# A buffer of its own for the experts' weighted rows, and the gate's Silu and product scheduled with priority

## The chip, the cores and the metric

The kernel runs on one core of a Trainium2 chip. The metric is the device time of one execution in microseconds (us), as the median of several runs. One execution was also profiled; all rows below come from that one.

## The reference, cut to what matters

The layer is a mixer (attention and a chunked recurrence) followed by an expert-choice mixture of experts. Only the experts matter here:

```python
# one of 16 experts e; each takes its own 128 tokens (the context's share included)
xe   = h2[idx[e]]                       # gather 128 rows of 1024
hid  = silu(xe @ w_gate[e]) * (xe @ w_up[e])     # 1024 x 1024 each
y    = (hid @ w_down[e]) * gate[e] * g2          # 1024 x 1024
acc.at[idx[e]].add(y)                   # scatter-add into the residual stream
```

All of it is float32. TensorE multiplies in a reduced form, so the kernel splits each operand into a high and a low part and forms three products (high by high, high by low, low by high).

## The kernel before, in words

The stage of the experts runs from about 1090 to 1680 us of the span. For each expert e, `up(e)` brings in four pairs of 1 MB pieces of `w_gate` and `w_up`, and `down(e-1)` four pieces of `w_down`: 12 loads of 1 MB per expert, all on SyncE's queue (L1469), each into a slot `raw` of a ring of 16 (RING 9, MORE 6 and one of the router's). Each piece holds two 128x1024 slices. For each slice ScalarE copies the high part `whi` (L1475) and VectorE subtracts to get the low part `wlo` (L1476), so that an expert needs 24 of each. The five `whi` and five `wlo` buffers (WHI, WLO) are the whole distance by which these two engines can run ahead of TensorE.

TensorE does 144 matmuls of 128x512 columns per expert: 96 into the PSUM banks `pgu` and `pgv` (the gate's and the up product), 48 into `py` (the down product), each triple by `mm3` (L172 high by high, L173 with the low part of the rows, L174 with the low part of the weights). Beside them it transposes the gathered rows `xe` of the next expert (8 transposes L1493 into `ptm`, then `xTh` on ScalarE, L177, and `xTl` on VectorE, L178) and the hidden rows `hid` (8 more, then `hTh` and `hTl`). `ptm` has two buffers, so four transposes must be read out by VectorE before the next four but four can start.

When `pgu` is complete, ScalarE writes Silu of it into `hid` (L1520, two halves), and VectorE multiplies by `pgv` (L1521, two halves). `pgu` has one buffer: the next expert's first matmul waits for that Silu. When `py` is complete, VectorE forms the weighted rows `y` (L1540), and GpSimd scatter-adds them to DRAM (L1541). Here `y` shares its one buffer with `hid` (YT): Silu of an expert may write only when the scatter of the preceding `y` has read it, and `y` only when `hid` was transposed. GpSimd also gathers the next `xe` (L1499) and builds the `onehot` tiles for the token lists of the expert after that (L1427), which TensorE reduces in `pls` (L1430).

The order of all instructions is set by a scheduler that plays the program through ahead of time with costs of its own, and takes on each engine the next ready instruction, by priority and program order. Each engine then executes its list strictly in that order. Code under `tc.high_priority()` is taken ahead of other ready work. What can move instructions is therefore also the number of buffers, not only the priority.

Of the kernel before, what the change touches and what calls it, by code (L numbers as in the profile page):

```python
# [18 lines left out]
F32 = mybir.dt.float32  # L19
# [3 lines left out]
AF = mybir.ActivationFunctionType  # L23
ALU = mybir.AluOpType
# [4 lines left out]
P = 128  # L29
D = 1024  # L30
# [36 lines left out]
PRIO2 = 1  # L67
FPOOL = (1,)
PRIO = 1000
MORE = 6  # L70
WAIT = (16, 17, 18)
YT, RT = "hid", "xe"
WHI, WLO = 5, 5
AT = 3
QP, WP = (3,), (1, 3, 5)
XKT, WMB, LATE = (3, 4), 4, (3, 7)
# [1372 lines left out]
def _experts(K, ring, route):  # L1449
    tc, nc, a = K.tc, K.nc, K.a  # L1450
    ident = K.cst(C_IDENT)
    with tc.tile_pool(name="m", bufs=1, side="right", reuse_waits="tile") as pm, \
# [3 lines left out]
        for nm in ("hTh0", "hTl0", "hTh1", "hTl1"):  # L1456
            pm.tile([P, 4, P], F32R, name=nm)
        ring.extend((pm, MORE), (route.keep, 1))
        pm.tile([P, 2, FF], F32, name="raw", bufs=MORE)

        loads = []

        def weights(w, e, j):
            raw = ring.tile()
            loads.append(raw)
            if len(loads) in WAIT:

                nc.gpsimd.tensor_copy(raw[:, 0, 0:1], ready[0][1])
            nc.sync.dma_start(raw, w[0, e].rearrange("(k p) f -> p k f", p=P)[:, 2 * j:2 * j + 2])  # L1469
            eng = nc.gpsimd if e == 0 and (j == 0 or w is a["w_gate"] and j == 1) else nc.vector  # L1470
            his, los = [], []
            for i in range(2):
                hi = pm.tile([P, FF], F32R, name="whi", bufs=WHI)
                lo = pm.tile([P, FF], F32R, name="wlo", bufs=WLO)
                nc.scalar.activation(hi, raw[:, i], AF.Copy)  # L1475
                eng.tensor_tensor(lo, raw[:, i], hi.bitcast(F32), ALU.subtract)  # L1476
                his.append(hi)
                los.append(lo)
            return his, los
# [7 lines left out]
        def turned(src, j, nm):  # L1487

            hi, lo = (pm.tile([P, 4, P], F32R, name=f"{nm}{x}{j}") for x in "hl")
            p = ps.tile([P, 4, P], F32, name="ptm", tag="ptm", bufs=2)  # L1490
            for i in range(4):
                c = (4 * j + i) * P
                nc.tensor.transpose(p[:, i], src[:, c:c + P], ident)  # L1493
            K.split(hi, lo, p)
            return hi, lo

        def gather(e):
            xe = pm.tile([P, D], F32, name="xe")
            nc.gpsimd.indirect_dma_start(out=xe, out_offset=None, in_=K.h2_dram,  # L1499
                                         in_offset=bass.IndirectOffsetOnAxis(ap=ready[e][0][:, :1], axis=0))  # L1500
            return xe

        def up(e, xT, xe):
            pg = [ps.tile([P, FF], F32, name=nm) for nm in ("pgu", "pgv")]
            nxt = []
            for j in range(4):
                ws = [first.pop(0) if first else weights(a[w], e, j) for w in ("w_gate", "w_up")]
                for m in range(2):
                    for i in range(2):
                        k = 2 * j + i  # L1510
                        for f in range(2):
                            fs = slice(f * 512, (f + 1) * 512)
                            K.mm3(pg[m][:, fs], *(x[:, k % 4] for x in xT[k // 4]), ws[m][0][i][:, fs], ws[m][1][i][:, fs],
                                  k == 0, k == KT - 1)
                if j % 2 and xe is not None:
                    nxt.append(turned(xe, j // 2, "xT"))
            hid = pm.tile([P, FF], F32, name="hid", tag="hid" if e + 1 < NE else "xe")
            for f in range(2):
                fs = slice(f * 512, (f + 1) * 512)
                nc.scalar.activation(hid[:, fs], pg[0][:, fs], AF.Silu)  # L1520
                nc.vector.tensor_tensor(hid[:, fs], pg[1][:, fs], hid[:, fs], ALU.mult)  # L1521
            return hid, nxt

        def down(e, hT, hid=None):
# [11 lines left out]
            return py, nxt  # L1536

        def scatter(e, py):
            y = pm.tile([P, D], F32, name="y", tag=YT)
            nc.vector.scalar_tensor_tensor(y, py, ready[e][1], gt2, op0=ALU.mult, op1=ALU.mult)  # L1540
            nc.gpsimd.indirect_dma_start(out=K.acc_dram, in_=y, in_offset=None, compute_op=ALU.add,  # L1541
                                         out_offset=bass.IndirectOffsetOnAxis(ap=ready[e][0][:, :1], axis=0))

        xe = gather(0)
# [3 lines left out]
        for e in range(NE):  # L1548
            xe = gather(e + 1) if e + 1 < NE else None
            if e + 2 < NE:  # L1550
                ready.append(route.lists(e + 2, ps))
            hid, xT = up(e, xT, xe)
            if e:
                if e + 1 == NE:
                    last_hT = [turned(hid, j, "xT") for j in range(2)]
                    hid = None
                py, hT = down(e - 1, hT, hid)
                scatter(e - 1, py)
            else:
                hT = [turned(hid, j, "hT") for j in range(2)]  # L1560
# [13 lines left out]
        def norm(xs, name, pool=()):  # L1574
            ss = pm.tile([P, len(xs)], F32, name="ss" + name)
            for i, x in enumerate(xs):
                nc.scalar.activation(junk, x, AF.Square, accum_out=ss[:, i:i + 1])
            nc.vector.tensor_scalar(ss, ss, 1.0 / D, EPS, op0=ALU.mult, op1=ALU.add)
            rs = K.rsqrt(pm, ss, len(xs), tag=name)
            for i, x in enumerate(xs):  # L1580
                if i in pool:
                    nc.scalar.activation(x, x, AF.Copy, scale=rs[:, i:i + 1])
                    nc.gpsimd.tensor_tensor(x, x, g, ALU.mult)
                else:
                    nc.vector.scalar_tensor_tensor(x, x, rs[:, i:i + 1], g, op0=ALU.mult, op1=ALU.mult)
# [6 lines left out]
            for t in range(t0, t0 + n):  # L1592
                nc.sync.dma_start(out[t * P:(t + 1) * P], acc[t])
        with tc.high_priority():
            y = pm.tile([P, D], F32, name="y", tag=YT)
            nc.vector.scalar_tensor_tensor(y, py, ready[last][1], gt2, op0=ALU.mult, op1=ALU.mult)
            nc.vector.tensor_tensor(rows, rows, y, ALU.add)
            norm([rows], "r")
            nc.gpsimd.indirect_dma_start(out=out, in_=rows, in_offset=None,
                                         out_offset=bass.IndirectOffsetOnAxis(ap=ready[last][0][:, :1], axis=0))  # L1600


def body(tc, a, taps=None, stop=None):
    nc = tc.nc
    K = _K(tc, a, taps)
    with tc.tile_pool(name="const", bufs=1) as pc, tc.tile_pool(name="dram", bufs=1, space=DRAM) as dr:
# [28 lines left out]
        with contextlib.ExitStack() as banks:  # L1635
            K.gps = [banks.enter_context(tc.tile_pool(name="gps", bufs=1, space=PSUM, reuse_waits="tile"))]
            prep, left = _inproj(K, banks)
            _mix(K, prep, left)
        ring, route, keep = _outproj(K)
        _experts(K, ring, route)  # L1640
        keep.close()

# [38 lines left out]
```

## Time and profile before

| | us |
|---|---|
| median of 3 runs | 1718.07 (1716.43 to 1720.74) |
| the profiled execution | 1718.15 |
| its span | 1716.4 |
| outside the span | 1.75 |

| engine | busy us | share of the span |
|---|---|---|
| TensorE (PE) | 1528.0 | 89% |
| its weight loads (PEld) | 1298.4 | 76% |
| VectorE (DVE) | 1309.4 | 76% |
| ScalarE (ACT) | 918.6 | 54% |
| GpSimd (POOL) | 637.6 | 37% |

In the stage of the experts TensorE is busy nearly all the time and VectorE not much less; the shares of the whole span hide this, since the stages ahead have other limits. A chain of waits, read backwards from the last instruction, tells which engine sets the end: 54% of it is TensorE's. "issue" in such a chain is time in which an engine waited for nothing that the profile shows.

### The profile page before, as it was taken

What the parts mean: (1) busy time and instruction counts of PE and PEld (TensorE: products, weight loads), DVE (VectorE), ACT (ScalarE), POOL (GpSimd) and SP (SyncE); (2) the same over time, 40 slices, a digit from 0 to 9 for tenths busy, and PEclk for the clock granted to TensorE, in tenths of its full rate; (3) what the DMA queues carried; (4) which work ended last, traced back from release to release, by engine and by line L of the source; (5) the groups of instructions that cost most, each with busy time, mean ns of one, the idle gap of its engine ahead of it and who ended that gap; (6) DMA issues with size and microseconds to landing.
All of it is one profiled execution on the core that took longest, in us unless ns stands there. A gap on an engine that the chain in (4) does not pass through costs nothing.

```text
span 1716.4 us, 24735 instructions
## 1 busy us (share of the span) xinstructions
PE 1528.0 (89%) x8793; PEld 1298.4 (76%) x8793; DVE 1309.4 (76%) x2110; ACT 918.6 (54%) x1514; POOL 637.6 (37%) x555
## 2 busy tenths in 40 slices
PE   6999889899978999999898994699999999999890
PEld 2897668787867988888887784578888777777780
DVE  6656754687768877778896546789999999898884
ACT  6521125334423656556574322387777777777773
POOL 3013331322235783483710115137644335450012
PEclk9999999999988999999999997799999999999995
DMA  7477953443655043414033766799999999999915
GB/s 263 168 246 233 268 144 107 144 133 113 183 171 159 24 104 95 113 52 145 32 105 103 229 240 232 261 342 378 399 396 398 397 359 363 358 371 373 347 25 220
DMA packets 170847, 377.17 MB, mean 220 GB/s; under 512 B 32542, under 2 KB 82140, under 8 KB 169572
## 3 DMA queue, kind: packets, MB, share of 16 engines
q1 hardware_dynamic: 131874, 315.22, 50.7%
q0 software_dynamic: 11664, 43.52, 8.6%
q10 hardware_dynamic: 27186, 16.86, 3.8%
q8 instruction: 69, 1.13, 0.3%
q14 instruction: 54, 0.44, 0.1%
HBM read 315.60 MB, written 55.76 MB: 216 GB/s over the span
## 4 chain that ended last, share of the span: by engine, by line
PE 54%; DVE 10%; POOL 4%; ACT 3%; DMA 3%; issue 3%; SPq 1%; POOLq 0%; ACTq 0%; DVEq 0%
PE pgu L172 4%; PE pgu L173 3%; PE pgu L174 3%; PE pgv L172 3%; PE pgv L174 3%; PE pgv L173 3%; PE py L172 3%; PE py L173 3%; PE py L174 3%; PE po L1068 2%; PE ptm L1493 2%; DVE mx L1043 2%; PE sp L1040 2%; PE pl L172 1%; PE pl L174 1%
## 5 line engine op out<-in xcount | busy, mean ns | idle before, releaser
L1476 DVE TENSOR_TENSOR wlo<-raw,whi 128x1024 fp32r<-128x1024 f32 x376 | 453.5, 1242 | 43.2 <-ACT whi L1475 35.1
L1475 ACT ACTIVATE whi<-raw 128x1024 fp32r<-128x1024 f32 x384 | 399.4, 1059 | 135.3 <-PE pgu L173 53.4
L1427 POOL TENSOR_SCALAR onehot<-fcst,slot 128x128 bf16<-128x128 f32 x96 | 158.8, 2047 | 43.0 <-PE pls L1430 22.6
L173 PE MATMUL pl<-XH,wl 128*128 128x512 f32 x384 | 152.5, 397 | 4.7 <-DVE wl L178 4.7
L172 PE MATMUL pl<-XH,wh 128*128 128x512 f32 x384 | 153.2, 399 | 0.9 <-DVE ab L413 0.9
L174 PE MATMUL pl<-XL,wh 128*128 128x512 f32 x384 | 153.0, 398 | 0.0
L1541 POOL DMA_INDIRECT acc_dram<-y,idx x15 | 36.1, 2410 | 280.0 <-DVE y L1540 266.0
L172 PE MATMUL pgu<-whi,xTh 128*128 128x512 f32 x256 | 103.3, 403 | 18.3 <-ACT hid L1520 18.3
L1046 ACT ACTIVATE pt<-sp,mx 128x1280 f32<-128x1280 f32 x64 | 84.9, 1326 | 56.3 <-DVE mx L1043 55.8
L1043 DVE TENSOR_REDUCE mx<-sp 128x1 f32<-128x1280 f32 x64 | 95.0, 1484 | 19.6 <-PE sp L1041 19.3
L174 PE MATMUL pgu<-wlo,xTh 128*128 128x512 f32 x256 | 102.6, 401 | 0.0
L172 PE MATMUL pgv<-whi,xTh 128*128 128x512 f32 x256 | 101.6, 397 | 0.0
L173 PE MATMUL pgu<-whi,xTl 128*128 128x512 f32 x256 | 101.5, 396 | 0.0
L174 PE MATMUL pgv<-wlo,xTh 128*128 128x512 f32 x256 | 100.8, 394 | 0.0
L173 PE MATMUL pgv<-whi,xTl 128*128 128x512 f32 x256 | 99.8, 390 | 0.0
L174 PE MATMUL py<-wlo,hTh 128*128 128x512 f32 x240 | 94.6, 394 | 0.7 <-POOL wlo L1476 0.7
L172 PE MATMUL py<-whi,hTh 128*128 128x512 f32 x240 | 93.9, 391 | 0.0
L173 PE MATMUL py<-whi,hTl 128*128 128x512 f32 x240 | 93.6, 390 | 0.0
L173 PEld LDWEIGHTS pl<-XH,wl 128*128 128x128 f32 x384 | 73.1, 190 | 21.5 <-DVE wl L178 5.4
L172 PEld LDWEIGHTS pl<-XH,wh 128*128 128x128 f32 x384 | 73.2, 191 | 20.3 <-issue 5.2
L1068 PE MATMUL po<-V,aT 128*128 128x128 f32 x640 | 87.9, 275 | 0.0
L1040 PE MATMUL sp<-KH,QS 128*128 128x512 f32 (+1 forms) x192 | 76.2, 397 | 11.1 <-ACT pt L1046 5.6
(542 smaller groups left out, 4025.6 us busy)
## 6 DMA issues: line engine op xcount, KB each, us to landing
raw<-w_gate SPq DMA_DIRECT2D x64, 1024.0 KB
raw<-w_up SPq DMA_DIRECT2D x64, 1024.0 KB
raw<-w_down SPq DMA_DIRECT2D x64, 1024.0 KB
rwm<-w_mod POOLq DMA_DIRECT2D x32, 512.0 KB, 6.5
wr<-w_in ACTq DMA_DIRECT2D x24, 512.0 KB
wm<-w_mod SPq DMA_DIRECT2D x8, 1024.0 KB
KH<-qk_dram SPq DMA_DIRECT2D x16, 320.0 KB
xt<-x SPq DMA_DIRECT2D x8, 512.0 KB
```

Of the source, the lines that this page charges most:

```text
L172: nc.tensor.matmul(out, ah, bh, start=start, stop=False)
L173: nc.tensor.matmul(out, al, bh, start=False, stop=False)
L174: nc.tensor.matmul(out, ah, bl, start=False, stop=stop)
L1040: nc.tensor.matmul(sp[:, k0:k1], qs, st["KH"][s][:, k0:k1], start=True, stop=False)
L1043: nc.vector.tensor_reduce(mx, sp[:, :LT], axis=AX.X, op=ALU.max, negate=True)
L1046: nc.scalar.activation(pt, sp[:, :LT], AF.Exp, bias=mx, accum_out=sm)
L1068: nc.tensor.matmul(po, aT[c], st["V"][:, c], start=c == 0, stop=c == NTT - 1)
L1427: eng.tensor_scalar(oh[:, t], iota, slot[:, t, e:e + 1], None, op0=ALU.is_equal)
L1475: nc.scalar.activation(hi, raw[:, i], AF.Copy)
L1476: eng.tensor_tensor(lo, raw[:, i], hi.bitcast(F32), ALU.subtract)
L1493: nc.tensor.transpose(p[:, i], src[:, c:c + P], ident)
L1541: nc.gpsimd.indirect_dma_start(out=K.acc_dram, in_=y, in_offset=None, compute_op=ALU.add, out_offset=bass.IndirectOffsetOnAxis(ap=ready[e] ...
```

## The change

Three constants and two places of `_experts` change. `y` loses its shared tag and gets a buffer of its own (4 KB of each partition). There is one `whi` buffer more (4 KB), and one ring slot `raw` fewer (8 KB), so the ring has 15 slots. Silu and its product stand under `tc.high_priority()`. No arithmetic changes. Lines behind the edit shift by one: Silu is L1521 after, the product L1522, `y` L1541, the scatter L1542.

```diff
-MORE = 6
+MORE = 5
 WAIT = (16, 17, 18)
-YT, RT = "hid", "xe"
-WHI, WLO = 5, 5
+RT = "xe"
+WHI, WLO = 6, 5
...
             for f in range(2):
                 fs = slice(f * 512, (f + 1) * 512)
-                nc.scalar.activation(hid[:, fs], pg[0][:, fs], AF.Silu)
-                nc.vector.tensor_tensor(hid[:, fs], pg[1][:, fs], hid[:, fs], ALU.mult)
+                with tc.high_priority():
+                    nc.scalar.activation(hid[:, fs], pg[0][:, fs], AF.Silu)
+                    nc.vector.tensor_tensor(hid[:, fs], pg[1][:, fs], hid[:, fs], ALU.mult)
...
         def scatter(e, py):
-            y = pm.tile([P, D], F32, name="y", tag=YT)
+            y = pm.tile([P, D], F32, name="y")
...
         with tc.high_priority():
-            y = pm.tile([P, D], F32, name="y", tag=YT)
+            y = pm.tile([P, D], F32, name="y")
```

The order of the instructions moves with it; Silu's place does from expert 6 on. ScalarE's list at expert 11, before: `hid` is the Silu of that expert, `xTh_14062` and `xTh_14159` are the rows of expert 12, `hTh_14218` and `hTh_14271` the hidden rows of expert 11.

```order
L1475 ACTIVATE whi<-raw 128x1024 x11
L177 ACTIVATE xTh_14062<-ptm 128x512
L1475 ACTIVATE whi<-raw 128x1024 x2
L177 ACTIVATE xTh_14159<-ptm 128x512
L1475 ACTIVATE whi<-raw 128x1024 x8
L1520 ACTIVATE hid<-pgu 128x512 x2
L1475 ACTIVATE whi<-raw 128x1024 x3
L177 ACTIVATE hTh_14218<-ptm 128x512
L177 ACTIVATE hTh_14271<-ptm 128x512
```

The same stretch of ScalarE's list after:

```order
L1475 ACTIVATE whi<-raw 128x1024 x11
L1521 ACTIVATE hid<-pgu 128x512 x2
L1475 ACTIVATE whi<-raw 128x1024 x10
L177 ACTIVATE xTh_14062<-ptm 128x512
L177 ACTIVATE xTh_14159<-ptm 128x512
L177 ACTIVATE hTh_14218<-ptm 128x512
L1475 ACTIVATE whi<-raw 128x1024 x3
L177 ACTIVATE hTh_14271<-ptm 128x512
```

Before, Silu stands behind copies that take the buffers of the last `py` matmuls. After, it stands ahead of ten copies, and both `xTh` of the next expert stand behind those ten. The early experts (1 to 5 before, 1 to 7 after) have another pattern, the same in both kernels: Silu directly after `pgu`, and both `xTh` amid an expert.

TensorE's list where expert 12 begins, before (`hTh_13936` is the second half of the hidden rows of expert 10, `xTh_14062` the first half of the rows of expert 12):

```order
L172 MATMUL py<-whi,hTh_13936 128x512
L173 MATMUL py<-whi,hTl_13937 128x512
L174 MATMUL py<-wlo,hTh_13936 128x512
L172 MATMUL pgu<-whi,xTh_14062 128x512
L173 MATMUL pgu<-whi,xTl_14063 128x512
L174 MATMUL pgu<-wlo,xTh_14062 128x512
```

And after:

```order
L172 MATMUL py<-whi,hTh_13936 128x512
L173 MATMUL py<-whi,hTl_13937 128x512
L174 MATMUL py<-wlo,hTh_13936 128x512
L1493 MATMUL ptm<-ident,xe 128x128 x8
L172 MATMUL pgu<-whi,xTh_14062 128x512
L172 MATMUL pgv<-whi,xTh_14062 128x512
L1493 MATMUL ptm<-ident,hid 128x128 x4
L173 MATMUL pgu<-whi,xTl_14063 128x512
```

The eight transposes of the next expert's rows moved from the middle of the up products to the place between two experts, and the first hidden transposes follow after two matmuls.

VectorE's list after, from the end of expert 10's up products to the start of expert 12 (the first `hid` pair is expert 10's product, the second expert 11's):

```order
L1476 TENSOR_TENSOR wlo<-raw,whi 128x1024 x10
L1541 SCALAR_TENSOR_TENSOR y<-py,gate,gt_10139 128x1024
L1522 TENSOR_TENSOR hid<-pgv,hid 128x512 x2
L1476 TENSOR_TENSOR wlo<-raw,whi 128x1024 x12
L178 TENSOR_TENSOR xTl_13728<-ptm,xTh_13727 128x512
...
L1476 TENSOR_TENSOR wlo<-raw,whi 128x1024 x9
L1541 SCALAR_TENSOR_TENSOR y<-py,gate,gt_10139 128x1024
L1476 TENSOR_TENSOR wlo<-raw,whi 128x1024 x3
L1522 TENSOR_TENSOR hid<-pgv,hid 128x512 x2
L1476 TENSOR_TENSOR wlo<-raw,whi 128x1024 x9
L178 TENSOR_TENSOR xTl_14063<-ptm,xTh_14062 128x512
```

The product stood behind all eight `wlo` of `w_down` before. After, in expert 10 seven of the eight stand behind it and one ahead; in experts 11 to 15 four stand ahead and four behind. `y` of an expert comes later in the next one than before. On GpSimd the scatter of `y` now stands ahead of the gather of `xe`, and the gather last, where before it was onehots, gather, scatter. SyncE's list of loads is the same.

## Rows read from the trace of the kernel before

**Rows 1.** Busy time, clock and DMA by 40 us stretches of the experts.

```profile
core 0: us, PE busy (x) PEld busy (x) DVE busy (x) ACT busy (x) POOL busy (x), PEclk, DMA share, GB/s
1180.00:1220.00 40.00, 40.00 (x194) 33.01 (x193) 38.30 (x40) 31.48 (x35) 19.38 (x11) 1.00 1.03 398
...
1380.00:1420.00 40.00, 37.84 (x180) 30.95 (x179) 36.09 (x39) 30.04 (x32) 17.02 (x13) 1.00 1.00 365
...
1460.00:1500.00 40.00, 37.84 (x174) 30.76 (x173) 34.85 (x36) 28.39 (x31) 17.45 (x11) 0.96 0.95 354
```

**Rows 2.** VectorE's timeline, rows of `y`: start us, us, what, idle before.

```profile
1260.52 1.28 DVE L1540 SCALAR_TENSOR_TENSOR y<-py,gate,gt 128x1024 f32<-128x1024 f32 x1 [0.23 <-PE py L174]
...
1295.31 1.28 DVE L1540 SCALAR_TENSOR_TENSOR y<-py,gate,gt 128x1024 f32<-128x1024 f32 x1 [0.51 <-PE py L174]
...
1408.20 1.28 DVE L1540 SCALAR_TENSOR_TENSOR y<-py,gate,gt 128x1024 f32<-128x1024 f32 x1
...
1445.55 1.29 DVE L1540 SCALAR_TENSOR_TENSOR y<-py,gate,gt 128x1024 f32<-128x1024 f32 x1
...
1484.45 1.28 DVE L1540 SCALAR_TENSOR_TENSOR y<-py,gate,gt 128x1024 f32<-128x1024 f32 x1 [0.16 <-PE ptm L1493]
...
1596.31 1.28 DVE L1540 SCALAR_TENSOR_TENSOR y<-py,gate,gt 128x1024 f32<-128x1024 f32 x1
...
1634.75 1.28 DVE L1540 SCALAR_TENSOR_TENSOR y<-py,gate,gt 128x1024 f32<-128x1024 f32 x1 [0.17 <-PE ptm L1493]
```

**Rows 3.** Waits in the experts' stage: engine, line, releaser: total us, times, longest.

```profile
ACT whi L1475 <- PE pgu L173: 53.4, 94, 2.6
...
PE pgu L172 <- ACT hid L1520: 18.3, 9, 2.2
```

**Rows 4.** The chain of waits between experts 7 and 8: start us, us, what.

```profile
1362.43 0.24 PE py L173
...
1362.69 0.04 ACT whi L1475
...
1363.66 1.04 ACT whi L1475
1364.70 0.98 ACT hid L1520 x2
...
1365.72 0.50 PE pgu L172
1366.22 0.23 PE pgu L173
```

**Rows 5.** Groups of instructions, 1180 to 1620 us: count, busy us, mean ns, idle before.

```profile
L1476 DVE TENSOR_TENSOR wlo<-raw,whi 128x1024 fp32r<-128x1024 f32 x293 | 350.4, 1229 | 31.3 <-ACT whi L1475 24.1 <-PE pgv L174 1.6
...
L178 DVE TENSOR_TENSOR xTl<-ptm,xTh 128x512 fp32r<-128x512 f32 x25 | 17.1, 682 | 0.0
...
L1540 DVE SCALAR_TENSOR_TENSOR y<-py,gate,gt 128x1024 f32<-128x1024 f32 x12 | 15.4, 1283 | 2.2 <-PE py L174 1.2 <-PE ptm L1493 0.2
L1521 DVE TENSOR_TENSOR hid<-pgv,hid 128x512 f32<-128x512 f32 x23 | 14.8, 682 | 1.4 <-ACT whi L1475 1.4
L177 ACT ACTIVATE xTh<-ptm 128x512 fp32r<-128x512 f32 x25 | 14.6, 583 | 0.5 <-PE ptm L1493 0.5
```

**Rows 6.** TensorE's timeline: eight transposes of one expert's rows.

```profile
1233.07 1.03 PE L1493 MATMUL ptm<-ident,xe 128*128 128x128 f32 x8
```

**Rows 7.** Waits of SyncE's queue, 1180 to 1340 us.

```profile
SPq L1469 <- DVE wlo L1476: 136.6, 56, 4.2
```

**Rows 8.** The gathered tile `xe`, 1180 to 1620 us.

```profile
DMA to landing us min/median/max: 7.6/8.1/9.0
```

**Rows 9.** The chain behind the gap at expert 11: matmuls at the lower clock.

```profile
1477.57 0.80 PE pgu L172
1478.37 0.43 PE pgu L173
...
1481.24 0.23 PE pgu L174
```

## The prediction

> **What bounds the kernel now.** I read the stretches first, then the times of `y`, then the waits, then the chain at one border between two experts. The reader is to see two regimes. Early on TensorE is busy 40.00 us of 40, and one expert takes 1295.31 - 1260.52 = 34.8 us. Later it is busy 37.84 of 40, and an expert takes 1445.55 - 1408.20 = 37.35 us [rows 1, 2]. The work is the same, so a late expert loses 2.5 us. The waits name the place: `pgu`, held by Silu, nine times, up to 2.2 us [rows 3]. One of the nine is expert 1's; the other eight are the starts of experts 8 to 15. The chain shows how [rows 4]: a `py` matmul ends and frees a `whi` buffer, two copies follow (the second ends at 1364.70), Silu takes 0.98 us, and `pgu` starts at 1365.72. Silu had long been possible, since `pgu` was full half an expert before; it stood in ScalarE's list behind copies that waited for `py`.
>
> VectorE is nearly as full: 38.30 of 40 us in the early regime [rows 1]. Whatever stops it for more than 4% of an expert comes through to TensorE.
>
> **The change part by part.** The sum goes against the profiled 1718.15 us (span 1716.4 and 1.75 outside it), which is practically the median of the runs, 1718.07.
>
> *Experts 8 and 9.* In the new order the early pattern lasts to expert 7, and at the start of expert 9 Silu is ahead of the last copies as well. Both gaps go: 2 x 2.5 = 5.0 us.
>
> *Experts 10 to 15, the border.* Silu no longer stands here. But both `xTh` of the next expert now do, and the eight transposes of its rows stand directly after `py`. Take the border of rows 4: the copies end at 1364.70 as before; then `xTh` instead of Silu, 0.58 us [rows 5], so `pgu` can start at about 1365.32, 0.40 earlier. In the gap TensorE does eight transposes, 1.03 us [rows 6], that it had to do elsewhere before. Against that, after two matmuls (2 x 0.23) it needs a free `ptm`, which VectorE's `xTl` releases 0.68 us after `xTh` [rows 5]: 0.2 us lost. Saved: 0.40 + 1.03 - 0.2 = 1.2 us, so 1.3 of the 2.5 us remain. Bounds: the whole 2.5 (if the copies come early enough) and nothing (if the wait only changes its name). I take 1.2, which is worked out from the nearest rows; 6 x 1.2 = 7.2 us.
>
> *Experts 9 and 10, the middle: a new wait.* Here Silu stands ahead of all eight copies for `w_down` and waits for the last `pgu` matmul, which is twelve matmuls (12 x 0.23 = 2.8 us) ahead of the last `pgv` matmul. Count from that last one: Silu ends at -1.8, the first copy at -0.7, its `wlo` (1.23 us [rows 5]) at +0.5. In expert 9 the product follows, two halves of 0.68, to 1.9, and the second `wlo` to 3.1. TensorE wants that one at eight matmuls after the last `pgv`, at 1.84: 1.3 us lost. In expert 10 `y` (1.28 us [rows 5]) stands in between too: 2.5 us lost. Behind the product on VectorE are the seven other `wlo` of `py`, for which TensorE waits; they come every 1.2 us and are used every 1.37, so that the loss does not grow. In experts 11 to 15 four `wlo` stand ahead of the product, 5.5 us of matmuls, which cover its 1.36 us and one more `wlo`. Cost 3.8 us; bounds 0 (the engines are further ahead than I count) and 2.5 in every expert from 9 on, 17.5.
>
> *The clock.* After two of the eight gaps the matmuls took 0.43 us instead of 0.23 [rows 9], and the granted clock of that stretch was 0.96 [rows 1]. Those two experts took 38.90 and 38.44 us [rows 2], 2.6 us together above a late expert without it. Half as long a gap in six places, and two new ones: bounds 0 and 2.6, I take half, 1.3.
> [...]
>
> *The ring, one slot less.* SyncE's loads waited for a free slot 56 times, 136.6 of 160 us [rows 7], so the ring is full, and no wait in the stage names a load. With 15 slots the lead is still over ten loads. Cost 0. If that cover were gone, ScalarE would wait for a load; the early regime already moved 398 GB/s [rows 1], which is what 34.8 us per expert need.
>
> *The sixth `whi`.* ScalarE waits 53.4 us for buffers that `pgu` frees [rows 3], but TensorE shows no wait for `whi`; a buffer more lets ScalarE run ahead and VectorE not. Nothing either way, between a part of the 1.3 us at the borders and zero.
>
> *`y` and GpSimd.* Own buffer: `y` needs no longer wait for the hidden rows, nor Silu for the scatter. The scatter now stands ahead of the gather. In the late pattern the gather has to wait for the transposes at the border anyway, lands at most 9.0 us later [rows 8], and its rows are wanted at the next border, some 33 us on. Over 20 us of cover; without it the price would be these 9 us. The last `y`, the final gather and the norm follow `py` in the same order as before: 0.
>
> *Sum:* -5.0 - 7.2 + 3.8 - 1.3 = -9.7; 1718.15 - 9.7 = 1708.4 us.
>
> **The rivals.**
>
> A, all late gaps go. If the sixth `whi` and the earlier Silu let ScalarE be done with the copies before `py` ends, the late experts run as the early ones: 8 x 2.5 + 2.6 = 22.6 us less, 1695.5. For it: the early experts show that 40.00 of 40 is possible. Against: the order puts two copies that need `py`'s last buffers ahead of `xTh`.
> [...]
>
> B, the wait only changes its name. The border keeps 2.5 us with `xTh` and `xTl` in Silu's place, because the copies or VectorE come later than in rows 4. Then -5.0 + 3.8 = -1.2: 1717, no change. For it: `xTh`, `ptm` and `xTl` are a chain of three engines, each with its latency. Against: 1.03 us of transposes lie in that gap for certain.
>
> C, slower: the product stops VectorE in every late expert. It stands in VectorE's list early, waits for the last `pgv`, and nothing behind it may pass. If ScalarE is late in experts 11 to 15 too, so that the four `wlo` ahead of the product are not done before `pgv` ends, each loses what expert 10 does: -8.4 + 5 x 2.5 = +4.1, with no clock regained; with two gaps per expert instead of one (13 in place of 8) the clock's 2.6 us become 4.3, +1.7: 1724. It decides from about 2.4 us per expert on. For it: VectorE has only 1.7 us of 40 to spare at full pace [rows 1]. Against: 5.5 us of cover by the order.
>
> **How the numbers follow.** My forecast 0.58, within 1703 to 1714; A 0.16; B 0.16; C 0.10. A measurement here can tell 0.3%, or 5.2 us: below 1712.9 is faster, above 1723.2 slower. Faster: 0.55 of the forecast's and A's 0.16, 0.71. Same: 0.03 and most of B and a third of C, 0.20. Slower: the rest of C and some mishap of B's, 0.09. The range goes from A's time to just past B's, 1696 to 1718; C and the outer part of A are left out.
>
> **What would show it.** In the changed profile `y` should come every 34.8 us up to expert 9 and every 36.2 in the last five experts. The wait of `pgu` for Silu should be gone but for expert 1, and one of `pgu` for `xTh`, about 0.9 us, and of `ptm` for `xTl`, about 0.2, stand in its place five or six times. `py` should wait for `wlo` twice, 1.3 and 2.5 us, near 1430 and 1470. I am wrong if `pgu` still waits for Silu, if `py` waits for `wlo` in every expert (C), if TensorE is busy 40 of 40 to the end (A), or if any copy waits for a load.

## The result: 1708.98 us, 0.6% less

| | before | after |
|---|---|---|
| median, range (5 runs each) | 1718.07 (1712.17 to 1720.74) | 1708.98 (1705.73 to 1713.00) |
| ratio, 95% interval | | 0.9938 [0.9915, 0.9961] |
| profiled execution | 1718.15 | 1713.00 |
| its span | 1716.4 | 1711.2 |
| start of the first `pgu` matmul to start of the last `py` matmul | 1092.2 to 1674.7: 582.5 | 1097.8 to 1670.3: 572.6 |

1708.4 was forecast. The profiled execution of after is the slowest of its five: its first `pgu` matmul starts 5.6 us later than before's, though up to there TensorE and VectorE do the same in both. The stages ahead of the experts vary by some us from run to run: the same changed kernel, profiled a second time, starts its first `pgu` at 1092.8 instead of 1097.8. So the length of the experts' stage, read off the timeline from the start of the first `pgu` to the start of the last `py` matmul, is the finer measure. It is 9.9 us shorter, against 9.7 forecast.

The stretches of after (the columns of [rows 1]):

```profile
1180.00:1220.00 40.00, 40.00 (x192) 32.88 (x191) 37.43 (x39) 31.91 (x37) 16.90 (x10) 1.00 1.03 383
...
1380.00:1420.00 40.00, 40.00 (x192) 33.04 (x192) 38.21 (x40) 31.70 (x34) 16.28 (x11) 1.00 1.03 395
1420.00:1460.00 40.00, 38.64 (x182) 30.88 (x181) 33.72 (x35) 26.45 (x30) 16.17 (x9) 1.00 0.98 365
1460.00:1500.00 40.00, 37.10 (x170) 29.71 (x169) 34.71 (x37) 29.91 (x33) 14.61 (x13) 0.96 0.97 361
1500.00:1540.00 40.00, 39.18 (x187) 31.95 (x186) 37.47 (x39) 31.78 (x35) 16.12 (x11) 1.00 1.02 379
...
1580.00:1620.00 40.00, 39.18 (x181) 32.06 (x180) 37.03 (x36) 31.37 (x33) 3.81 (x2) 1.00 1.02 382
```

The early regime, TensorE 40.00 of 40, now lasts to 1420 us, where it had ended by 1380 [rows 1]. Then come two stretches with stalls, one of them at a lower clock, and a new steady state at 39.18 instead of 37.84. Waits of the stage, where [rows 3] stood:

```profile
ACT whi L1475 <- PE pgu L173: 36.7, 82, 2.6
...
PE pgu L172 <- ACT xTh L177: 4.2, 6, 0.8
...
PE py L172 <- DVE y L1541: 1.9, 1, 1.9
...
PE py L174 <- DVE wlo L1476: 0.9, 2, 0.7
...
PE pgu L172 <- ACT hid L1521: 0.7, 1, 0.7
...
PE ptm L1493 <- DVE xTl L178: 0.4, 2, 0.2
```

ScalarE waits 36.7 us for buffers that `pgu` frees, where it waited 53.4. Of the 18.3 us for Silu 0.7 is left, at expert 1; `xTh` has taken Silu's place with 4.2 us, `py` waits twice for a low part and once for `y`, and no copy waits for a load. The chain at the start of expert 12, which answers to [rows 4]:

```profile
1513.95 0.24 PE py L173
...
1514.21 0.02 ACT whi L1475
...
1515.18 1.04 ACT whi L1475
1516.22 0.49 ACT xTh L177
...
1516.75 0.50 PE pgu L172
1517.25 0.23 PE pgv L172
...
1517.51 0.66 PE ptm L1493 x4
```

The copies still end 2.3 us behind the start of that `py` matmul (1516.22), then `xTh` takes 0.49 and `pgu` starts. The eight transposes, which the chain doesn't name, lie in the gap (1514.92 to 1515.95).

### The profile page after: what moved, and what is told of

It is laid out like the page before. It is cut to its first block, busy times and chain, and to the rows that moved or that the text cites. A ratio compares the mean times of both kernels' runs of the same rounds, so it can differ in the third digit from the quotient of the medians.

```text
span 1711.2 us, 24881 instructions
## 1 busy us (share of the span) xinstructions
PE 1533.0 (90%) x8793; PEld 1301.3 (76%) x8793; DVE 1309.0 (76%) x2110; ACT 917.8 (54%) x1514; POOL 618.7 (36%) x555
## 4 chain that ended last, share of the span: by engine, by line
PE 55%; DVE 9%; issue 4%; ACT 3%; DMA 3%; POOL 3%; SPq 0%; POOLq 0%; DVEq 0%; ACTq 0%
PE pgu L172 4%; PE pgu L174 3%; PE pgu L173 3%; PE pgv L173 3%; PE pgv L174 3%; PE pgv L172 3%; PE py L172 3%; PE py L173 3%; PE py L174 3%; PE po L1068 3%; PE pp L172 2%; PE pp L173 2%; PE sp L1040 2%; DVE mx L1043 2%; PE pp L174 1%
## 5 line engine op out<-in xcount | busy, mean ns | idle before, releaser
L1476 DVE TENSOR_TENSOR wlo<-raw,whi 128x1024 fp32r<-128x1024 f32 x376 | 448.7, 1238 | 31.2 <-ACT whi L1475 10.0
L1475 ACT ACTIVATE whi<-raw 128x1024 fp32r<-128x1024 f32 x384 | 399.0, 1060 | 105.7 <-PE py L173 36.9
L1427 POOL TENSOR_SCALAR onehot<-fcst,slot 128x128 bf16<-128x128 f32 x96 | 140.5, 1477 | 156.8 <-PE pls L1430 156.8
L174 PEld LDWEIGHTS pl<-XL,wh 128*128 128x128 f32 x384 | 73.4, 191 | 15.6 <-issue 0.9
```

The source lines that it names most:

```text
L174: nc.tensor.matmul(out, ah, bl, start=False, stop=stop)
L1427: eng.tensor_scalar(oh[:, t], iota, slot[:, t, e:e + 1], None, op0=ALU.is_equal)
```

## The experiments

Each was timed in turns with the kernel before on the same chip, in five rounds; a ratio is to the kernel before there. The stage is the length as above, of the profiled execution.

| kernel | ratio, 95% interval | stage, us |
|---|---|---|
| before | 1 | 582.5 |
| after | 0.9938 [0.9915, 0.9961] | 572.6 |
| priority alone | 0.9997 [0.9979, 1.0014] | 583.0 |
| `y` of its own alone | 0.9952 [0.9929, 0.9974] | 575.2 |
| two `xe`, `y` of its own | 1.0033 [1.0018, 1.0048] | 587.8 |
| two `xe`, `y` shared | 1.0010 [0.9993, 1.0027] | 582.5 |
| two `y` | 0.9988 [0.9962, 1.0014] | 585.1 |
| two `y`, two `xe` | 0.9937 [0.9913, 0.9962] | 574.4 |
| the same, six `whi` | 0.9952 [0.9933, 0.9970] | 575.2 |
| the same, six `whi`, six `wlo` | 0.9924 [0.9897, 0.9951] | 569.8 |
| three slots fewer | 0.9991 [0.9970, 1.0012] | 582.4 |
| sixth `whi` alone | 0.9995 [0.9973, 1.0016] | 582.5 |
| after, once more | 0.9913 [0.9882, 0.9943] | 572.6 |

The stages of the kernels that keep before's gaps lie within 0.6 us, and that of the changed kernel came out the same twice, while whole runs of the kernel before spread over some 15 us on one chip. Each of these stages also holds the falls of the clock in its own execution, stretches in which a matmul takes 0.43 us instead of 0.23; one costs about 1.6 us (shown below).

**Which part of the change does it.** Priority alone:

```diff
-                nc.scalar.activation(hid[:, fs], pg[0][:, fs], AF.Silu)
-                nc.vector.tensor_tensor(hid[:, fs], pg[1][:, fs], hid[:, fs], ALU.mult)
+                with tc.high_priority():
+                    nc.scalar.activation(hid[:, fs], pg[0][:, fs], AF.Silu)
+                    nc.vector.tensor_tensor(hid[:, fs], pg[1][:, fs], hid[:, fs], ALU.mult)
```

> The kernel before with nothing changed but Silu and its product under priority (shared buffer, 16 slots and five whi kept). Theory (the buffer does it): Silu was late because its output buffer was not free, not because other work was taken ahead of it; priority moves nothing, and on every engine the order is that of the kernel before, row for row. Expected: 1718 us, ratio 1.000 within 0.003, pgu waiting for Silu nine times, some 18 us. Rival (priority does it): the wait of pgu for Silu is gone and the time is near 1709. Its ratio also shows how far two programs of one order differ on the chip.

It is the same program: on all five engines the lists agree row for row, and the wait of `pgu` is that of before.

```profile
PE pgu L172 <- ACT hid L1521: 18.3, 9, 2.2
```

Likewise the changed kernel without the priority is built to the lists of the changed kernel, row for row; it was not run. `y`'s buffer alone (cut to what matters, as are the edits below):

```diff
-MORE = 6
+MORE = 5
...
-            y = pm.tile([P, D], F32, name="y", tag=YT)
+            y = pm.tile([P, D], F32, name="y")
```

> The changed kernel without the priority and without the sixth whi (15 slots, five whi, y in its own buffer). Theory (the buffer does it): the wait of pgu for Silu goes as in the changed kernel. By its order the transposes of the next rows stand between two experts only from expert 12 on, so four borders of 1.3 us remain of eight gaps of 2.5, with perhaps one stall of 2 us where the pattern turns: 1718.1 - 22.6 + 4 x 1.3 + 2 = 1702.7, a few us below the changed kernel. Rival (the sixth whi has a share in the gain): 1712 to 1718, with ScalarE or TensorE waiting longer for whi than in the changed kernel.

0.9952: most of the gain is there without priority and without the sixth `whi`. Since the priority moves nothing, the sixth `whi` is what separates this kernel from the changed one. With it the stage is 2.6 us shorter, with one fall of the clock in each of the two; in the ratios, whose intervals overlap, that can't be told. What TensorE waits for in this kernel:

```profile
PE ptm L1493 <- DVE xTl L178: 3.2, 4, 0.8
...
PE pgu L172 <- ACT xTh L177: 2.6, 4, 0.8
...
PE py L174 <- DVE wlo L1476: 2.0, 5, 0.7
...
PE py L172 <- DVE y L1540: 2.0, 1, 2.0
```

The wait for Silu is gone. The size was missed by 8 us of stage (7.3 shorter instead of 15.4): each of the last borders has two waits of up to 0.8 us, and an expert there takes 36.6 to 36.9 us, some 1.9 above an early one, where I had put 1.3; in the experts where the pattern turns `py` meets late low parts in three and a late `y` in a fourth, and behind that `y` the clock fell (granted 0.98 from 1500 to 1600 us, 1.00 in the 100 us ahead and the 60 us after). The sixth `whi` alone:

```diff
-MORE = 6
+MORE = 5
...
-WHI, WLO = 5, 5
+WHI, WLO = 6, 5
```

> The kernel before with 15 slots and a sixth whi, y still in the buffer of hid, no priority. By its order Silu stands behind as many copies of the next expert as before. Theory 1 (what held Silu were copies that wait for the last py matmuls): with six buffers the last copy ahead of Silu waits for a matmul about 1.1 us earlier, so pgu still waits for Silu at the start of each late expert, but 1.2 instead of 2.3 us: 9 us less, ratio 0.995. Theory 2 (the sixth whi is worth nothing, as predicted): 1.000 within 0.003 and gaps of 2.3 us.

Nothing, though by another way than I thought. The chain at the start of expert 8:

```profile
1363.47 0.24 PE py L173
...
1363.73 0.02 ACT whi L1475
...
1364.70 1.04 ACT whi L1475
1365.74 0.98 ACT hid L1520 x2
...
1366.76 0.50 PE pgu L172
```

Again the two copies ahead of Silu are behind the last `py` matmuls, and `pgu` starts 3.29 us behind the start of that `py` matmul, as in [rows 4]. Counted in ScalarE's list, the Silu of a late expert e stood behind 24e + 21 copies; with six buffers it stands behind 24e + 22. The scheduler uses the new buffer to put one more copy ahead of Silu. My expectation took the order as fixed ("behind as many copies as before"), which was a miscount; theory 1 so got no test of its own.

Three ring slots fewer:

```diff
-MORE = 6
+MORE = 3
```

> The kernel before with three ring slots fewer (13 instead of 16) and nothing else, 24 KB left empty. Theory (the ring is full and only its lead shrinks): 1.000 within 0.003, no copy waits for a load. Rival (every slot counts): slower, with ScalarE waiting for raw loads.

No change in time. Against what I expected two copies now wait for a load, 1.1 us together, where none did before; the queue waits for slots as before, and its wait in the changed kernel is 136.6 us too.

```profile
PE pgu L172 <- ACT hid L1520: 17.9, 9, 2.2
...
ACT whi L1475 <- DMA raw<-w_down: 1.1, 2, 0.8
```

```profile
SPq L1469 <- DVE wlo L1476: 134.4, 55, 4.2
```

```profile
SPq L1469 <- DVE wlo L1476: 136.6, 55, 3.7
```

(The last of the four rows is of the changed kernel, the others of 13 slots; the queue's rows are of 1180 to 1340 us.) So a ring slot was free to give away.

**Which wait comes next.** A second buffer for the gathered rows, beside `y`'s own:

```diff
-            xe = pm.tile([P, D], F32, name="xe")
+            xe = pm.tile([P, D], F32, name="xe", bufs=2)
...
```

> As the run with only y's own buffer, and the 4 KB that the sixth whi took go to a second buffer for the gathered rows xe, so that a gather need not wait for the transposes of the rows before. By its order the early pattern (both xTh amid an expert) then lasts to expert 14. Theory (the border that is left is xTh behind the copies, because the rows come late): no gap between experts, TensorE busy 40 of 40 to about 1640 us, y every 34.8 us, clock 1.00: 1718.1 - 22.6 = 1695.5. Rival (VectorE, 38.3 of 40 us, is then the bound): gaps move to py or pgu waiting for wlo and the time stays at 1702 or above.

Slower than before, and neither theory holds: the rival had the time right (1702 or above) but named the wrong wait. `xTh` does stand amid the expert to the end. But from 1480 us on TensorE waits for this:

```profile
PE py L172 <- DVE y L1540: 10.7, 5, 4.0
PE ptm L1493 <- DVE xTl L178: 4.7, 2, 2.9
PE ptm L1493 <- DVE hid L1521: 3.0, 3, 1.3
```

`y` drifts through VectorE's list until it stands nearly an expert late, and `py`, which has one buffer, can't start before `y` has read it: up to 4.0 us. Falls of the clock come on top, behind the longest of these gaps: 0.91 was granted from 1540 to 1580 us and 0.96 in each of the next two stretches of 40 us, where it was 1.00 from 1100 to 1540. I had compared only ScalarE's list. The same with `y` shared:

```diff
-RT = "xe"
+YT, RT = "hid", "xe"
...
-            y = pm.tile([P, D], F32, name="y")
+            y = pm.tile([P, D], F32, name="y", tag=YT)
```

> The second xe buffer without y's own: y shares the buffer of hid as before, 15 slots, five whi (4 KB left empty). Theory (the shared buffer makes Silu late, whatever the gather does): Silu still stands behind the copies for py, pgu waits for it from expert 8 on, 2.2 us each; 1718, ratio 1.000 within 0.004. Rival (the late gather is the root of both patterns): most of the gaps go and the time is below 1708.

```profile
PE pgu L172 <- ACT hid L1520: 17.9, 9, 2.2
```

As expected: with the shared buffer Silu is late whatever the gather does. Two buffers for `y`, one `xe`:

```diff
-            y = pm.tile([P, D], F32, name="y")
+            y = pm.tile([P, D], F32, name="y", bufs=2)
```

> As the run with only y's own buffer (15 slots, five whi, one xe), but y has two buffers. Theory (in the changed kernel y stands late in VectorE's order because its one buffer comes free only when the scatter before has read it, and the py bank that y has not read yet holds TensorE in the middle of an expert): with two, y stands within the first quarter of an expert again, the 2.1 us in front of py where the pattern turns is gone, and the borders of 0.9 + 1.0 us from expert 12 on stay. About 3 us below the run with one y, ratio to the kernel before 0.993. Rival (the middle stalls come from the product standing in front of the copies' low parts): nothing changes, 0.995.

The wait of `py` for `y` is gone, as the theory said. The gain is not: in VectorE's list `y` now stands at the border itself, ahead of `xTl`. TensorE's waits from 1500 us on, and VectorE's timeline at one border:

```profile
PE ptm L1493 <- DVE xTl L178: 9.1, 4, 3.0
PE pgu L172 <- ACT xTh L177: 2.6, 4, 0.8
```

```profile
1551.06 1.28 DVE L1540 SCALAR_TENSOR_TENSOR y<-py,gate,gt 128x1024 f32<-128x1024 f32 x1 [1.17 <-PE py L174]
1552.26 3.49 DVE L1476 TENSOR_TENSOR wlo<-raw,whi 128x1024 fp32r<-128x1024 f32 x3
1555.66 1.28 DVE L178 TENSOR_TENSOR xTl<-ptm,xTh 128x512 fp32r<-128x512 f32 x2
```

`y` starts at 1551.06, three low parts follow, and `xTl` only at 1555.66, so that the hidden transposes wait up to 3.0 us for a free `ptm`. Behind each of these four waits the clock fell: 0.95 was granted from 1500 to 1600 us and 0.97 from 1600 to 1660, where it was 1.00 from 1100 to 1500. The stretch of the second:

```profile
1540.00:1580.00 40.00, 36.22 (x167) 29.29 (x166) 34.03 (x35) 27.65 (x31) 3.61 (x2) 0.96 1.00 362
```

Two `y` and two `xe` together, then the same with `WHI` 6 alone, and last with six of each (the second edit is to the first):

```diff
-MORE = 5
+MORE = 4
...
-            xe = pm.tile([P, D], F32, name="xe")
+            xe = pm.tile([P, D], F32, name="xe", bufs=2)
...
-            y = pm.tile([P, D], F32, name="y")
+            y = pm.tile([P, D], F32, name="y", bufs=2)
```

> Two buffers for y and two for the gathered rows xe, five whi, 14 slots. Theory (two late things hold the late experts: the rows, which put xTh between two experts, and y, which holds py): neither is late any more, the early pattern lasts to the end, no gap over 0.5 us, TensorE 40 of 40 us up to about 1640, clock 1.00 throughout: 22 us less than before, ratio 0.987. Rival (VectorE is the bound as soon as the gaps go): py and pgu wait for wlo, ratio 0.993 or above. Rival (14 slots are too few): copies wait for loads.

> As the run with two y and two xe, with a sixth whi in the 4 KB that are left. Theory (TensorE never waits for whi): same time as with five, 0.987, within 0.3%. Rival (the sixth whi is worth something once the gaps are gone): 0.985 or below.

```diff
-MORE = 4
+MORE = 3
...
-WHI, WLO = 5, 5
+WHI, WLO = 6, 6
```

> Two y, two xe, six whi and six wlo, 13 slots. By its order the product stands behind one low part of w_down, as with five. Theory (the order, not the depth, makes py wait for the second low part behind the product): the 0.37 + 0.38 us in the middle of each expert from 8 on stay, ratio 0.994. Rival (a sixth wlo lets VectorE be ahead and cover the product): the stalls go, 0.989 or below.

No gap is left at the borders, and yet the time is that of the changed kernel, 10.7 us below the kernel before and not 22, with six `whi` much as with five (9.8 us below). The rival was right in what waits: the product now stands in front of the second low part of `w_down` in every expert from 8 on, as in expert 9 of the changed kernel. It is the order that makes VectorE late there; full it is not, with 36.74 and 36.43 of 40 us in the stretches below. With six of each, from 1380 us on:

```profile
PE py L174 <- DVE wlo L1476: 4.1, 17, 0.7
```

Seventeen waits, two per expert, each up to 0.7 us, and the stretches never lower than 39.3:

```profile
1460.00:1500.00 40.00, 39.34 (x189) 31.34 (x188) 36.74 (x39) 29.99 (x35) 14.16 (x10) 1.00 1.02 386
1540.00:1580.00 40.00, 39.57 (x187) 31.80 (x186) 36.43 (x39) 27.07 (x33) 9.72 (x2) 1.00 1.01 379
```

Depth did not remove these stalls, as the order's theory said. An expert in the middle of this stretch takes about 36.2 us from start to start, 1.2 more than an early one. The waits come to only 0.5 of that, since a row of waits leaves out what follows: behind such a wait of the changed kernel the next matmul starts 0.34 us later (1429.81 to 1430.15) instead of 0.23. Two longer stalls at the end, the longest 2.1 us with five of each, are gone; the lists moved there as well, so that depth alone is not shown to have done it. The stage is 569.8 us, 4.6 shorter than with five and 2.8 shorter than the changed kernel's, of which 1.6 is the one fall of the clock there (with six of each the granted clock is 1.00 in all stretches from 1380 to 1650 us). In whole times that can't be told: 1707.62 us beside 1706.21 of the changed kernel on the same chip. No version that I ran beats the changed kernel beyond the noise.

> The changed kernel again, on the chip of the two others. Theory: 0.994 as at first, no gap before expert 9, 0.9 us at each border from expert 10 on. It is there so that the versions are compared on one chip.

It repeats: 0.9913, whose interval overlaps the first, gaps of the same length at the same places, and the fall of the clock at the same expert.

## Why the prediction was right, point by point

Read from the start of one expert's first `pgu` matmul to another's, the stage can be set beside the terms of the sum:

| from the start of expert | before, us | after, us | difference | forecast, without the clock | falls to the lower clock |
|---|---|---|---|---|---|
| 0 to 6 | 200.29 | 199.76 | -0.5 | 0 | |
| 6 to 9 | 110.39 | 105.35 | -5.0 | -5.0 | none |
| 9 to 10 | 37.35 | 37.45 | +0.1 | +0.1 | none |
| 10 to 11 | 37.32 | 40.19 | +2.9 | +1.3 | one after |
| 11 to 15 | 150.36 | 144.27 | -6.1 | -4.8 | one before |
| 15 to the last `py` | 46.77 | 45.54 | -1.2 | 0 | one before |

Expert 11 before, with a fall, took 38.9 us where its neighbours took 37.3, so one fall costs about 1.6 us, and with it the terms fit one by one to 0.4 us. That the totals agree to 0.2 us is in part luck, since the 0.5 us of the first experts stood in no term.

*Experts 8 and 9, 5.0 us:* right. TensorE has no gap at the start of either.

*The border, 1.3 us left of 2.5:* right. Two neighbouring starts of `pgu`, at 1516.75 and 1552.87, are 36.12 us apart, 1.3 above 34.8. `xTh` took Silu's place: `pgu` starts 0.53 us behind the copies instead of 1.02, so 0.49 is saved where 0.40 was put in; the rest came with the transposes. The 0.2 us for `xTl` came out as 0.2 at expert 12 (the hidden transposes start 0.42 us behind the start of the `pgv` matmul, instead of 0.23) and as 0.3 to 0.5 at experts 11 and 10, where the pattern was still turning.

*Expert 9, 1.3 us:* right in place, cause and size. Silu waited for `pgu`, the copy for Silu, the product stood ahead of the second low part, and `py` waited twice, 0.37 and 0.84 us by the starts of the matmuls (0.9 in the row of waits):

```profile
1425.22 0.95 ACT whi L1475
...
1426.20 0.69 DVE wlo L1476
...
1427.34 0.79 DVE hid L1522 x2
...
1428.54 1.23 DVE wlo L1476
...
1429.81 0.50 PE py L174
```

*Expert 10, 2.5 us:* the place and nearly the size are right, the cause is not. The step that failed is "the second `wlo`" with `y` in between. TensorE did stop, for 2.1 us, but earlier in its list: at the first `py` matmul, since `y` had not yet read the one `py` buffer:

```profile
1462.52 0.95 ACT whi L1475
...
1463.50 0.69 DVE wlo L1476
...
1464.64 1.29 DVE y L1541
...
1466.07 0.47 PE py L172
...
1467.23 0.25 PE py L173
1467.48 0.43 PE py L174
1467.91 0.43 PE py L172
```

I had written `y` only as 1.28 us in VectorE's list, and of its lateness only that the scatter comes later; that `y` frees `py` was not in the sum. Here both give much the same. In the run with two `xe` the same thing decided the time, and there I had missed it again.

*The clock, half of 2.6 us:* came out at half, though by the starts a fall costs 1.6 us and not 1.3. One stretch fell instead of two, behind expert 10's 2.1 us (0.43 us matmuls in the chain above), and none behind a border, where the gaps are 0.8 us. That half as long a gap costs half was my estimate, and no run shows it: behind gaps under 2.0 us the clock did not fall at all. That the place changes with equal gaps is shown by two executions of one order, with eight gaps of 2.3 us each: the kernel before fell at experts 11 and 15, the run with priority alone at 9 and 15.

*Ring and sixth `whi`, nothing:* right for the kernel before, by the runs of 13 slots and of the sixth `whi` alone. Beside `y`'s own buffer the sixth `whi` shortens the profiled stage by 2.6 us. For `whi` my reason was wrong: a buffer more lets ScalarE run ahead only if the order does.

*The rivals.* A would have needed the borders without `xTh`; two `xe` and two `y` gave that and uncovered the product. The runs of priority alone (0.9997) and of the buffer alone (0.9952) show that the shared buffer held Silu. But a buffer more did not end the gap, it changed what the gap waits for. B happened by half: the wait did change its name, and 1.3 of the 2.5 us stayed, 0.8 of them in the row for `xTh`. C stayed out here; the version with two of each is bounded by a stall of its kind, with the product ahead of the second low part in every expert.

## What to carry to other kernels

Where a scheduler sets the order, a buffer is a move of instructions: look up in each engine's list what it displaces, and check all engines, since a fix read from one list alone (ScalarE's, for the second `xe`) made the kernel 0.3% slower than before, where without it it was 0.5% faster. Before crediting a priority, compare the two lists; here it moved nothing. And where other stages of a run vary by more than the change is worth, measure the changed stage by itself in the profile as well.

## What I had not expected of the hardware

In the thirteen profiled executions, from expert 1 on, the lower clock (matmuls 0.43 us apart instead of 0.23) came only behind gaps of 2.0 us or more (from the starts of neighbouring matmuls, less the 0.23 us that one takes), and only sometimes. Five executions have eight gaps of 2.3 us each, and two falls each: at experts 11 and 15 (before), 9 and 15 (priority alone), 8 and 14 (`xe` shared, and again 13 slots), 10 and 15 (sixth `whi`). The changed kernel fell once, at expert 10, behind its one gap of 2.1 us. Behind gaps under 2.0 us there was none; the shortest gap with a fall behind it was one of 2.0 us, with two `y`. What picks two of eight equal gaps, no run here shows.

The stages ahead of the experts took from 1090.4 to 1102.2 us to the first `pgu` matmul. One order alone gave 1092.2 and 1102.2 (the kernel before and priority alone), while the experts' stage repeated to 0.6 us; no run here shows what makes the difference.
